# Strassen operands of h read back from a float32 copy in memory, and the softplus chain moved behind the second slab pair

## The chip, the core and the metric

The kernel runs on one core of a Trainium2 chip. The metric is device time in microseconds (us). Five engines work side by side, each through its own list of instructions and strictly in that list's order: TensorE (PE: matmuls, with its weight loads shown as PEld), VectorE (DVE), ScalarE (ACT), GpSimd (POOL) and SyncE (SP), which here issues every transfer between memory and the chip. An instruction whose data is not there yet holds up everything behind it in its own list. The profile was taken from one execution of the kernel before the change.

## What is computed

One layer of a decoder trunk, for 1024 tokens (S) of width 1024 (D):

```
h      = rmsnorm(x, norm_w) * (1 + scale) + shift        # scale, shift from c
proj   = h @ w_in                                        # 1024 x 8472
z_ssm, xbc, dt_raw, q, k, v, z_att, f_logit, g_logit = split(proj)
dt     = softplus(dt_raw + dt_bias)                      # SSD branch, 16 heads
log_f  = log_sigmoid(f_logit + b_f)                      # attention branch, 8 heads
y_ssm  = ssd(silu(conv(xbc)), dt, ...) gated by z_ssm
y_att  = softmax attention with cumsum(log_f) gated by z_att
out    = rmsnorm(x + gate * ((g_ssm * y_ssm@Wp + g_att * y_att@Wa) @ Wo))
```

All of it is float32. TensorE multiplies a rounded form (fp32r), so each operand is split into a rounded part "hi" and a rest "lo", and a product is three matmuls: hi*hi, hi*lo, lo*hi.

## The kernel before

**First phase (L202 to L326).** x is normalised, transposed on TensorE in half tiles of 128 by 512 (L302), and turned into h by ScalarE (`xa`, L305). `xa` is then split: ScalarE casts the rounded part `hh` (L306), VectorE subtracts to get `hl` (L307). Eight tiles k = 0..7 of D, two halves each. The scale and shift come from matrix-vector products that VectorE does as chains of 128x256 multiply-adds on `w_ada` (L287, L289). TensorE uses `hh` and `hl` at once for three slabs of the gate projection (L115 to L117).

**Second phase (L607 to L614).** `v_slab(0)` computes two heads of v and, in 24 more columns, the raw dt and f values (L140 to L142); eight small VectorE copies (L348) take these columns out of the PSUM banks into `tmp`. `t_forms(k)`, k = 0..3, builds Strassen sums of h: four blocks of h (two of tile k, two of tile k+4) are made by adding `hh` and `hl` (L440: eight adds on VectorE, eight on GpSimd), four VectorE subtractions combine them (L441 to L444), and each result is split again (L102 cast on ScalarE, L103 subtraction on VectorE or GpSimd) into the tiles `tha, tla, thb, tlb`. `gate_slab(3)` is one more plain slab. Then `dt_chain` evaluates the softplus for all 24 columns: 28 VectorE instructions on 128x192 values with one ScalarE exponential, ending in two small TensorE matmuls (L393, L394) that sum over time; `ssm_sums` does the sums for the SSD branch (L401 to L427).

**Slab pairs (L616 to L627).** The other 34 slabs of the projection are done in pairs n = 0..16. A pair of slabs is one 2x2 Strassen product: seven products f1, f6, f7, f5, f4, f2, f3, each of 12 matmuls of 128x512, instead of eight. f1 and f2, f3 use `hh, hl`; f6 and f4 use `thb, tlb`; f7 and f5 use `tha, tla`. The weight sums are VectorE subtractions (L477 to L480), each followed by a cast (ScalarE) and a subtraction (GpSimd, L103). The results are combined by VectorE reading PSUM (L504 to L517). Pair 1 is a pair of convolution slabs: behind its products VectorE runs eight 128x1024 instructions (L538, L541, L544). `WPREP` says ahead of which pair the Strassen sums of later weights are prepared (`w_sums`, L586 to L594).

The eight PSUM banks are three `mm` and five `pp` tiles. The instructions are put in order when the program is built, by a scheduler that follows the code's order as its priority and hands out the tiles of a pool in the order in which the code asks for them. So a `pp` bank that a later product needs is only given out after the `pp` bank that an earlier statement asked for.

Of the kernel before, what the change touches and what calls it, by code (L numbers as in the profile page):

```python
# [31 lines left out]
P = 128  # L32
S = 1024
D = 1024
NK = 8
# [17 lines left out]
OOUT = (1, 2, 6, 7, 5, 4, 3)  # L53
WV = {'ps': (), 'pa': (1,), 'o': (1, 2, 3)}
WVI = (("o", 3),)
WPREP = {0: [('ps', 0)], 2: [('ps', 1)], 3: [('ps', 2)], 6: [('ps', 3), ('pa', 0)], 8: [('pa', 1)], 10: [('pa', 2), ('g', 0)], 12: [('pa', 3), ('g', 2), ('g', 3)], 11: [('g', 1)], 13: [('G', 0)], 15: [('o', 0)], 16: [('o', 1)], 17: [('o', 2)], 18: [('o', 3)]}
PREP = (6, 1, 0, 0, 0, 0, 0, 0, 1)
APRI, SPRI = 1000, 300
FILL = [[], [0, 2], [4, 5, 9], [1, 3, 6, 7, 8]]
# [10 lines left out]
def build(ctx, tc, t):  # L70
# [9 lines left out]
    def f32(ap):  # L80
        return ap.bitcast(F32)
# [120 lines left out]
    with tc.tile_pool(name="st", bufs=1, side="right") as st, \  # L202
# [95 lines left out]
        def h_half(k, hf):  # L298
            fs = slice(hf * 512, (hf + 1) * 512)
            tp = stp.tile([P, 512], F32, tag="tp", bufs=1, name="tp")  # L300
            for i in range(4):
                PE.transpose(out=tp[:, i * P:(i + 1) * P], in_=xts[4 * hf + i][:, k * P:(k + 1) * P],  # L302
                             identity=ident)
            xa = st.tile([P, 512], F32, tag="xa", bufs=4, name="xa")
            A.activation(out=xa, in_=tp, func=AF.Identity, scale=av[:, k:k + 1], bias=sv[:, k:k + 1])  # L305
            A.copy(out=hh[k][:, fs], in_=xa)  # L306
            V.tensor_tensor(out=hl[k][:, fs], in0=xa, in1=f32(hh[k][:, fs]), op=ALU.subtract)  # L307

# [24 lines left out]
    def gate_slab(j):  # L333
        evac, store = gate_out(j)
        c_slab(t["w_c"], G0 + j, hh, hl, evac)
        store()

    def v_slab(pair, dtf=None):
        vt = []

        def evac(tb, ps):
            per = ps.shape[1]
            g, i = tb // 4, tb % 4
            if i == 0:
                vt.append(ev("vt")[:, :1024].rearrange("p (i c) -> p i c", i=4))
            A.copy(out=vt[g][:, i:i + per, :], in_=ps[:, :, 0:256])
            if dtf is not None:
                V.tensor_copy(out=dtf[:, tb:tb + per, :], in_=ps[:, :, 256:280])  # L348
            if i + per == 4:
                SP.dma_start(out=v_scr[pair][g], in_=vt[g])  # L350

        if dtf is not None:
            with tc.issue_after(was["last"].ins):
                t_slab([t["w_v0"][u] for u in range(4)], 280, hh, hl, evac)
        else:
            t_slab([t["w_v"][pair - 1, u] for u in range(4)], 256, hh, hl, evac)
# [3 lines left out]
    with tc.tile_pool(name="pa", bufs=1, side="right") as pa, \  # L360
# [71 lines left out]
        def pe_tile():  # L432
            return pa.tile([P, 512], F32, tag="pe", bufs=4, name="pe")

        def t_forms(k):
            th1, tl1, th2, tl2 = (pa.tile([P, S], F32R, name=f"t{n}{k}") for n in ("ha", "la", "hb", "lb"))
            b11, b12, b21, b22 = (pe_tile() for _ in range(4))
            lo, hi = slice(0, 512), slice(512, 1024)
            for b, kk, hs, eng in ((b11, k, lo, V), (b12, k, hi, G), (b22, k + 4, hi, G), (b21, k + 4, lo, V)):
                eng.tensor_tensor(out=b, in0=f32(hh[kk][:, hs]), in1=f32(hl[kk][:, hs]), op=ALU.add)  # L440
            V.tensor_tensor(out=b11, in0=b12, in1=b11, op=ALU.subtract)  # L441
            V.tensor_tensor(out=b12, in0=b22, in1=b12, op=ALU.subtract)
            V.tensor_tensor(out=b22, in0=b22, in1=b11, op=ALU.subtract)
            V.tensor_tensor(out=b21, in0=b21, in1=b22, op=ALU.subtract)  # L444
            for b, th, tl, hs, eng in ((b11, th1, tl1, lo, V), (b12, th1, tl1, hi, G), (b22, th2, tl2, hi, V),
                                       (b21, th2, tl2, lo, G)):
                split(b, th[:, hs], tl[:, hs], 512, eng)
            tta.append((th1, tl1))
            ttb.append((th2, tl2))
# [157 lines left out]
        tmp = ev("tmp")  # L607
        dtf = tmp[:, 0:192].rearrange("p (c n) -> p c n", n=24)
        v_slab(0, dtf)
        for k in range(4):  # L610
            t_forms(k)
        gate_slab(3)
        dt_chain(dtf, tmp)
        ssm_sums()  # L614
        gb = None
        for n, (sa, sb) in enumerate(PAIRS):  # L616
            for wn, p in WPREP.get(n, ()):
                if wn == "g":
# [622 lines left out]
```

## Time and profile before

| | |
|---|---|
| median of 3 runs | 1285.14 us (1281.14 to 1290.57) |
| the profiled execution, its own time | 1286.09 us |
| its span, first to last instruction | 1284.4 us |
| mean granted TensorE clock | 0.974 |
| PE busy | 1183.9 us, 92% of the span |
| DVE busy | 963.1 us, 75% |
| POOL busy | 776.1 us, 60% |
| ACT busy | 594.8 us, 46% |

TensorE is the engine that is nearly always busy, so time is lost where TensorE waits. A row of a timeline gives the start, the duration, engine, line and operation, and in brackets the idle time ahead of it with the instruction that ended this idle time. A row of windows gives for each engine the busy time (and the count of instructions) in a stretch. Stretches here are in us from the span's start.

### The profile page before, as it was taken

How to read it: one execution, taken by the hardware profiler on the slowest of the kernel's cores; microseconds unless marked ns; L12 is line 12 of the kernel's file. 1: busy time of each engine (PE TensorE's matmuls, PEld its weight loads, DVE VectorE, ACT ScalarE, POOL GpSimd, SP SyncE). 2: the span in 40 equal slices, each digit the busy share in tenths (PEclk: the TensorE clock that was granted, in tenths of full speed). 3: DMA queues.
4: the chain of work that ended last, by engine and by line, in shares of the span. 5: the costliest groups of instructions: out<-in, count | busy, mean ns of one | idle time of the engine just before them, and what ended most of it. 6: DMA issues, size and time to landing. Idle time of an engine off the chain costs nothing. (4 is left out here: it accounts for less than half of the span.)

```text
span 1284.4 us, 18783 instructions
## 1 busy us (share of the span) xinstructions
PE 1183.9 (92%) x6206; PEld 988.8 (77%) x6206; DVE 963.1 (75%) x1618; ACT 594.8 (46%) x1194; POOL 776.1 (60%) x644
## 2 busy tenths in 40 slices
PE   4897899999978999999988999999999999999896
PEld 3686688777766788799778888888887787878685
DVE  6979767787799566348689764545667968999997
ACT  5443324242423232477667733444456553444354
POOL 3258465474755476448887966435446635587666
PEclk9998899998989999999999999999999999999999
DMA  8422443624556566654565558623236619766143
GB/s 346 158 100 98 160 123 124 213 64 167 188 185 216 175 211 228 223 177 148 188 200 163 173 191 296 210 87 116 74 127 210 201 55 328 224 188 193 52 116 145
DMA packets 104126, 219.70 MB, mean 171 GB/s; under 512 B 11818, under 2 KB 19420, under 8 KB 103004
## 3 DMA queue, kind: packets, MB, share of 16 engines
q1 hardware_dynamic: 104028, 218.50, 51.5%
q8 instruction: 49, 0.80, 0.3%
q14 instruction: 49, 0.40, 0.1%
HBM read 154.85 MB, written 63.61 MB: 170 GB/s over the span
## 5 line engine op out<-in xcount | busy, mean ns | idle before, releaser
L103 POOL TENSOR_TENSOR wl<-wr,wh 128x512 fp32r<-128x512 f32 (+1 forms) x188 | 281.5, 1508 | 135.7 <-ACT wh L102 130.7
L102 ACT CAST wh<-wr 128x512 fp32r<-128x512 f32 (+1 forms) x214 | 129.8, 618 | 158.4 <-DMA wr<-w_c 53.7
L103 POOL TENSOR_TENSOR sl<-sr,sh 128x512 fp32r<-128x512 f32 x57 | 91.0, 1603 | 78.8 <-ACT sh L102 65.7
L115 PE MATMUL mm<-hh,wh 128*128 128x512 f32 x288 | 115.9, 407 | 4.3 <-ACT wh L102 1.9
L116 PE MATMUL mm<-hl,wh 128*128 128x512 f32 x288 | 116.7, 405 | 3.0 <-DVE hl L307 3.0
L117 PE MATMUL mm<-hh,wl 128*128 128x512 f32 x288 | 116.3, 405 | 0.0
L102 ACT CAST sh<-sr 128x512 fp32r<-128x512 f32 x57 | 34.1, 619 | 96.6 <-DVE sr L478 77.0
L140 PE MATMUL mm<-wh,hh 128*128 128x256 f32 (+1 forms) x256 | 74.9, 294 | 3.8 <-DVE tmp L348 3.8
L141 PE MATMUL mm<-wl,hh 128*128 128x256 f32 (+1 forms) x256 | 74.8, 293 | 0.0
L142 PE MATMUL mm<-wh,hl 128*128 128x256 f32 (+1 forms) x256 | 74.4, 292 | 0.0
L1018 ACT ACTIVATE pr<-pr,sm 128x1024 f32<-128x1024 f32 (+3 forms) x64 | 49.9, 780 | 50.4 <-DVE sm L1017 42.4
L1021 POOL TENSOR_SCALAR pr<-pr,sm 128x1024 f32<-128x1024 f32 (+3 forms) x64 | 48.6, 762 | 34.7 <-DVE sm L1020 30.2
L1013 DVE CUSTOM_DVE_ANT_0 pr<-lg,fb 128x512 f32<-128x512 f32 (+1 forms) x96 | 51.5, 551 | 23.5 <-PE lg L1012 14.0
L115 PEld LDWEIGHTS mm<-hh,wh 128*128 128x128 f32 x288 | 55.1, 193 | 15.6 <-ACT wh L102 2.4
L116 PEld LDWEIGHTS mm<-hl,wh 128*128 128x128 f32 x288 | 55.3, 192 | 14.7 <-DVE hl L307 3.9
L1004 POOL TENSOR_SCALAR_AFFINE_SELECT fb<-fb 128x128 f32<-128x128 f32 x64 | 21.9, 344 | 72.1 <-DVE sm L1013 57.3
L117 PEld LDWEIGHTS mm<-hh,wl 128*128 128x128 f32 x288 | 55.2, 192 | 10.8
L1037 DVE TENSOR_TENSOR ptl<-tp,pth 128x512 fp32r<-128x512 f32 (+1 forms) x80 | 50.1, 632 | 15.9 <-ACT pth L1036 15.5
L1036 ACT CAST pth<-tp 128x512 fp32r<-128x512 f32 (+1 forms) x80 | 42.3, 543 | 41.5 <-PE tp L1033 32.4
L683 ACT ACTIVATE ab<-ab,acs 128x128 f32<-128x128 f32 x128 | 41.1, 391 | 31.7 <-DMA ab<-a_scr 28.1
L140 PEld LDWEIGHTS mm<-wh,hh 128*128 128x128 f32 x256 | 49.5, 194 | 4.7 <-DVE tmp L348 4.5
L103 POOL TENSOR_TENSOR m<-ab,m 128x512 fp32r<-128x512 f32 x32 | 46.7, 1462 | 7.1 <-ACT m L102 4.7
(393 smaller groups left out, 3972.6 us busy)
## 6 DMA issues: line engine op xcount, KB each, us to landing
wr<-w_c SPq DMA_DIRECT2D x116, 256.0 KB, 3.5
wa<-w_ada SPq DMA_DIRECT2D x8, 1024.0 KB, 11.4
g_scr<-gt SPq DMA_DIRECT2D x16, 512.0 KB, 4.0
ab<-a_scr SPq DMA_DIRECT2D x32, 256.0 KB, 3.7
gt<-g_scr SPq DMA_DIRECT2D x32, 256.0 KB, 3.0
wr<-w_ps SPq DMA_DIRECT2D x28, 256.0 KB, 2.9
wr<-w_pa SPq DMA_DIRECT2D x28, 256.0 KB, 3.1
wr<-so SPq DMA_DIRECT2D x28, 256.0 KB, 2.6
```

What stands on the lines that cost most here:

```text
L102: A.copy(out=hi[:, :n], in_=raw[:, :n])
L103: eng.tensor_tensor(out=lo[:, :n], in0=raw[:, :n], in1=f32(hi[:, :n]), op=ALU.subtract)
L115: PE.matmul(ps, lhsT=hi[:, cs], rhs=xh[k][:, hs], start=(k == 0), stop=False)
L116: PE.matmul(ps, lhsT=hi[:, cs], rhs=xl[k][:, hs], start=False, stop=False)
L117: PE.matmul(ps, lhsT=lo[:, cs], rhs=xh[k][:, hs], start=False, stop=(k == 7))
L140: PE.matmul(o, lhsT=xh[k][:, ts], rhs=hi[:, cs], start=(k == 0), stop=False)
L141: PE.matmul(o, lhsT=xh[k][:, ts], rhs=lo[:, cs], start=False, stop=False)
L142: PE.matmul(o, lhsT=xl[k][:, ts], rhs=hi[:, cs], start=False, stop=(k == 7))
L1013: V.tensor_tensor_reduce(out=pr[:, n0:n1], in0=lg[:, :n1 - n0], in1=fb[:, n0:n1], op0=ALU.add, op1=ALU.min, scale=1.0, scalar=BIG, accum_o ...
L1018: A.activation(out=pr[:, :n], in_=pr[:, :n], func=AF.Exp, scale=-1.0, bias=sm[:, 0:1], accum_out=sm[:, 1:2])
L1021: G.tensor_scalar(out=pr[:, :n], in0=pr[:, :n], scalar1=sm[:, 1:2], scalar2=0.5, op0=ALU.mult, op1=ALU.mult)
L1037: V.tensor_tensor(out=ptl[:, :w], in0=tp[:, :w], in1=f32(pth[:, :w]), op=ALU.subtract)
```

## The change

Five edits, all before the third slab pair:

- ScalarE's `xa` is also stored to a float32 copy of h in memory, `h_scr` (16 transfers of 256 KB).
- `t_forms` loads its four blocks from `h_scr` (16 transfers of 256 KB) in place of the 16 adds. For odd k the four blocks sit in buffers of the pool `sh` instead of `pe`.
- `gate_slab(3)` stands ahead of `t_forms`.
- The raw dt and f columns are stored to `d_scr`; `dt_chain` is called ahead of pair 2 on a copy that is loaded back, and `ssm_sums` ahead of pair 3.
- The first `w_sums` goes from pair 0 to pair 1.

```
-WPREP = {0: [('ps', 0)], 2: [('ps', 1)], ...
+WPREP = {1: [('ps', 0)], 2: [('ps', 1)], ...
...
+    h_scr = [dram.tile([P, S], F32, name=f"h_scr{k}") for k in range(NK)]
+    d_scr = dram.tile([P, 192], F32, name="d_scr")
...
             A.activation(out=xa, in_=tp, func=AF.Identity, scale=av[:, k:k + 1], bias=sv[:, k:k + 1])
+            SP.dma_start(out=h_scr[k][:, fs], in_=xa)
             A.copy(out=hh[k][:, fs], in_=xa)
...
         def t_forms(k):
-            b11, b12, b21, b22 = (pe_tile() for _ in range(4))
+            b11, b12, b21, b22 = (pe_tile() if k % 2 == 0 else pa.tile([P, 512], F32, tag="sh", bufs=SB[1], name="sb")
+                                  for _ in range(4))
             lo, hi = slice(0, 512), slice(512, 1024)
-            for b, kk, hs, eng in ((b11, k, lo, V), (b12, k, hi, G), (b22, k + 4, hi, G), (b21, k + 4, lo, V)):
-                eng.tensor_tensor(out=b, in0=f32(hh[kk][:, hs]), in1=f32(hl[kk][:, hs]), op=ALU.add)
+            for b, kk, hs in ((b12, k, hi), (b11, k, lo), (b22, k + 4, hi), (b21, k + 4, lo)):
+                SP.dma_start(out=b, in_=h_scr[kk][:, hs])
...
         v_slab(0, dtf)
+        SP.dma_start(out=d_scr, in_=tmp[:, 0:192])
+        gate_slab(3)
         for k in range(4):
             t_forms(k)
-        gate_slab(3)
-        dt_chain(dtf, tmp)
-        ssm_sums()
         gb = None
         for n, (sa, sb) in enumerate(PAIRS):
+            if n == 2:
+                tmp = ev("tmp")
+                SP.dma_start(out=tmp[:, 0:192], in_=d_scr)
+                dt_chain(tmp[:, 0:192].rearrange("p (c n) -> p c n", n=24), tmp)
+            if n == 3:
+                ssm_sums()
```

In the changed file the lines of the first phase stand 2 to 3 lower, those of `dt_chain` 3 (L393 is L396 there, L387 is L390) and those of the pairs 4 lower (L504 is L508, L541 is L545). The text below goes by the numbers of the kernel before.

The change also moves instructions in the engines' lists. Three places follow, of before and of the change apart.

TensorE's list around the first matmul of `dt_chain` (its operand is `tmp`), before: it stands inside the products of pairs 0 and 1 (`tha` with `wl` is f7 of pair 0, `thb` with `sh` into `mm` is f6 of pair 1, `tha` with `sh` into `pp` is f5 of pair 0).

```order
L497 MATMUL mm<-tha_1134,wl 128x512
L495 MATMUL mm<-thb_1064,sh 128x512
L393 MATMUL pp<-tri,tmp 64x128
L496 MATMUL mm<-tlb_1065,sh 128x512
L409 MATMUL pp<-a,tri 128x128
L410 MATMUL pp<-a,ones 128x128
L411 MATMUL pp<-tri,a 128x128
L495 MATMUL pp<-tha_1062,sh 128x512
L394 MATMUL pp<-ones,tmp 64x128
```

The same matmul after the change (L396), behind f7, f5 and f4 of pair 2 and ahead of f1 of pair 2.

```order
L499 MATMUL mm<-thb_1228,wh 128x512
L500 MATMUL mm<-tlb_1229,wh 128x512
L501 MATMUL mm<-thb_1228,wl 128x512
L396 MATMUL pp<-tri,tmp 64x128
L499 MATMUL pp<-hh_240,wh 128x512
L500 MATMUL pp<-hl_248,wh 128x512
L501 MATMUL pp<-hh_240,wl 128x512
```

So f1, f6, f2 and f3 of pair 2 now stand behind a matmul that needs the value written by L387 (L390 there), near the end of `dt_chain`; f7, f5 and f4 of pair 2 have gone ahead of them.

VectorE's list behind the last combination of pair 1 (L517), before: the convolution's instructions stand between those that combine pair 2 (L504 to L511).

```order
L517 TENSOR_TENSOR pp<-pp,pe 128x512
L477 TENSOR_TENSOR sr<-wr 128x512
L538 TENSOR_SCALAR cv<-xp,cols 128x1024 x2
L478 TENSOR_TENSOR sr<-sr,wr 128x512
L479 TENSOR_TENSOR wr<-wr 128x512
L541 SCALAR_TENSOR_TENSOR cv<-xp,cols,cv 128x1024 x2
L480 TENSOR_TENSOR sr<-wr,sr 128x512
L504 TENSOR_TENSOR pe<-pp,pe 128x512
L541 SCALAR_TENSOR_TENSOR cv<-xp,cols,cv 128x1024 x2
L505 TENSOR_TENSOR pe<-mm,pe 128x512
```

The same place after the change: from the combination (L521 is L517 of before) to the start of the softplus chain (L372 is L369).

```order
L521 TENSOR_TENSOR pp<-pp,pe 128x512
L591 TENSOR_TENSOR sr<-sr,wr 128x512
L542 TENSOR_SCALAR cv<-xp,cols 128x1024 x2
L545 SCALAR_TENSOR_TENSOR cv<-xp,cols,cv 128x1024 x4
L481 TENSOR_TENSOR sr<-wr 128x512
L545 SCALAR_TENSOR_TENSOR cv<-xp,cols,cv 128x1024 x2
L482 TENSOR_TENSOR sr<-sr,wr 128x512
L483 TENSOR_TENSOR wr<-wr 128x512
L548 SCALAR_TENSOR_TENSOR cv<-xp,cv 128x1024
L484 TENSOR_TENSOR sr<-wr,sr 128x512
L548 SCALAR_TENSOR_TENSOR cv<-xp,cv 128x1024
L372 TENSOR_TENSOR tmp<-tmp,hb 128x192
```

All of the convolution, then the whole chain, now precede the first combination of pair 2 (L508 there, not yet in these rows). The `tmp` of the chain takes the buffer of a convolution input, so its load too comes behind the first L544.

VectorE's list in the first phase, before: the `hl` of tile 4 (`hh_235`), and how many multiply-adds on `w_ada` still follow it.

```order
L307 TENSOR_TENSOR hl_243<-xa,hh_235 128x512
L289 SCALAR_TENSOR_TENSOR acc<-wa,cols,acc 128x256 x2
L307 TENSOR_TENSOR hl_243<-xa,hh_235 128x512
L289 SCALAR_TENSOR_TENSOR acc<-wa,cols,acc 128x256 x2
L307 TENSOR_TENSOR hl_244<-xa,hh_236 128x512
L289 SCALAR_TENSOR_TENSOR acc<-wa,cols,acc 128x256 x4
L307 TENSOR_TENSOR hl_244<-xa,hh_236 128x512
L289 SCALAR_TENSOR_TENSOR acc<-wa,cols,acc 128x256
```

After the change (L310 is L307, `hh_244` is tile 4, `hh_245` tile 5), down to the first instruction of `t_forms`.

```order
L291 SCALAR_TENSOR_TENSOR acc<-wa,cols,acc 128x256 x3
L310 TENSOR_TENSOR hl_252<-xa,hh_244 128x512
L296 SCALAR_TENSOR_TENSOR av<-cp,cols 128x1
L298 TENSOR_TENSOR sv<-cp,cols 128x1
L310 TENSOR_TENSOR hl_252<-xa,hh_244 128x512
L310 TENSOR_TENSOR hl_253<-xa,hh_245 128x512 x2
L310 TENSOR_TENSOR hl_254<-xa,hh_246 128x512 x2
L310 TENSOR_TENSOR hl_255<-xa,hh_247 128x512 x2
L445 TENSOR_TENSOR pe<-pe 128x512
```

The nine multiply-adds that followed the first `hl` of tile 4 now precede it.

More of the change, by code (lines that the diff above doesn't have):

```diff
@@ L55 @@
 WVI = (("o", 3),)
-WPREP = {0: [('ps', 0)], 2: [('ps', 1)], 3: [('ps', 2)], 6: [('ps', 3), ('pa', 0)], 8: [('pa', 1)], 10: [('pa', 2), ('g', 0)], 12: [('pa', 3), ('g', 2), ('g', 3)], 11: [('g', 1)], 13: [('G', 0)], 15: [('o', 0)], 16: [('o', 1)], 17: [('o', 2)], 18: [('o', 3)]}
+WPREP = {1: [('ps', 0)], 2: [('ps', 1)], 3: [('ps', 2)], 6: [('ps', 3), ('pa', 0)], 8: [('pa', 1)], 10: [('pa', 2), ('g', 0)], 12: [('pa', 3), ('g', 2), ('g', 3)], 11: [('g', 1)], 13: [('G', 0)], 15: [('o', 0)], 16: [('o', 1)], 17: [('o', 2)], 18: [('o', 3)]}
 PREP = (6, 1, 0, 0, 0, 0, 0, 0, 1)
```

## The prediction

> **What bounds the kernel now.** I read the engines' totals first, then windows of 20 us over the changed stretch, then the timelines of TensorE and VectorE there. The page's total, and behind it the windows (start:end, length, busy us and count for PE, PEld, DVE, ACT, POOL, then granted clock, DMA share, GB/s):
>
> ```profile
> PE 1183.9 (92%) x6206; PEld 988.8 (77%) x6206; DVE 963.1 (75%) x1618; ACT 594.8 (46%) x1194; POOL 776.1 (60%) x644
> ```
>
> ```profile
> 60.00:80.00 20.00, 20.00 (x111) 17.13 (x110) 9.86 (x17) 9.02 (x14) 3.43 (x2) 0.99 0.00 1
> 80.00:100.00 20.00, 16.52 (x124) 15.84 (x123) 18.85 (x18) 8.64 (x18) 17.19 (x11) 1.00 0.64 217
> 100.00:120.00 20.00, 16.18 (x76) 13.95 (x77) 19.28 (x22) 7.13 (x14) 16.18 (x10) 0.83 0.15 50
> 120.00:140.00 20.00, 15.28 (x59) 11.65 (x57) 19.76 (x27) 7.92 (x14) 13.71 (x11) 0.91 0.35 111
> 140.00:160.00 20.00, 18.64 (x77) 14.70 (x78) 12.49 (x31) 5.97 (x11) 8.85 (x7) 0.91 0.57 196
> 160.00:180.00 20.00, 20.00 (x89) 16.21 (x88) 9.64 (x13) 7.08 (x12) 11.99 (x9) 1.00 0.50 159
> ```
>
> TensorE is full up to 80 us and again from 160. From 80 to 160 it is busy 66.62 of 80, so 13.4 us are idle, and VectorE is busy 18.85 to 19.76 of 20 up to 140: there VectorE bounds the kernel, with `t_forms` and `dt_chain`. TensorE's timeline gives the marks:
>
> ```profile
> 56.58 0.50 PE L116 MATMUL mm<-hl,wh 128*128 128x512 f32 x1 [2.31 <-DVE hl L307]
> 79.33 0.39 PE L117 MATMUL um<-hh,e 128*128 128x512 f32 x1
> 100.34 0.40 PE L140 MATMUL mm<-wh,hh 128*128 128x280 f32 x1 [3.02 <-DVE tmp L348]
> 113.00 0.50 PE L115 MATMUL mm<-hh,wh 128*128 128x512 f32 x1 [1.93 <-ACT wh L102]
> 131.53 0.50 PE L495 MATMUL mm<-thb,sh 128*128 128x512 f32 x1 [3.87 <-ACT gt L186]
> 132.41 0.63 PE L495 MATMUL mm<-thb,sh 128*128 128x512 f32 x1
> 134.97 0.63 PE L495 MATMUL mm<-thb,sh 128*128 128x512 f32 x1
> 135.39 0.52 PE L496 MATMUL mm<-tlb,sh 128*128 128x512 f32 x1
> 141.36 0.43 PE L393 MATMUL pp<-tri,tmp 128*64 128x128 f32 x2 [2.21 <-DVE tmp L387]
> 155.94 0.39 PE L495 MATMUL pp<-hh,wh 128*128 128x512 f32 x1
> 156.17 0.39 PE L496 MATMUL pp<-hl,wh 128*128 128x512 f32 x1
> 174.69 0.39 PE L497 MATMUL pp<-hh,sl 128*128 128x512 f32 x1
> 194.09 0.40 PE L497 MATMUL pp<-hh,sl 128*128 128x512 f32 x1
> ```
>
> 156.17 - 155.94 gives the pitch, 0.23 us per 128x512 matmul (a modelled end makes a row longer). Pair 1 runs from 155.94 to 174.92 (19.0), pair 2 to 194.32 (19.4): 84 matmuls at 0.23, no gap. A gate slab of 48 is 11.2, a product of 12 is 2.8.
>
> **The change part by part.** All on the profiled execution's own time, 1286.09, which is 0.95 above the median of the three runs.
>
> *First phase.* Nine multiply-adds of L289 move ahead of the first `hl` of tile 4. VectorE's rows:
>
> ```profile
> 56.45 0.87 DVE L289 SCALAR_TENSOR_TENSOR acc<-wa,cols,acc 128x256 f32<-128x256 f32 x2
> 77.85 1.78 DVE L441 TENSOR_TENSOR pe<-pe 128x512 f32<-128x512 f32 x1
> 80.98 0.68 DVE L443 TENSOR_TENSOR pe<-pe 128x512 f32<-128x512 f32 x1
> 81.70 1.80 DVE L444 TENSOR_TENSOR pe<-pe 128x512 f32<-128x512 f32 x1
> 117.64 1.25 DVE L369 TENSOR_TENSOR tmp<-tmp,hb 128x192 f32<-128x192 f32 x1
> 134.43 0.35 DVE L379 SCALAR_TENSOR_TENSOR tmp<-tmp 128x192 f32<-128x192 f32 x1
> 175.12 0.70 DVE L517 TENSOR_TENSOR pp<-pp,pe 128x512 f32<-128x512 f32 x1 [2.10 <-PE pp L497]
> 178.58 1.10 DVE L477 TENSOR_TENSOR sr<-wr 128x512 f32<-128x512 f32 x1 [2.77 <-DMA wr<-w_c]
> 192.47 1.27 DVE L541 SCALAR_TENSOR_TENSOR cv<-xp,cols,cv 128x1024 f32<-128x1024 f32 x1
> 197.85 4.00 DVE L544 SCALAR_TENSOR_TENSOR cv<-xp,cv 128x1024 f32<-128x1024 f32 x2
> ```
>
> Nine at 0.45 (0.87 for two, with little overlap) are 4.1 us. TensorE already waits 2.31 for this `hl` at 56.58 and has no gap from there to 79.56, so all of it lands on the path: the phase ends near 83.7.
>
> *Loads in place of adds.* The 16 stores hold back nothing but SP, whose DMAs idle in that window (share 0.00 in 60:80). Four rows price the step: ScalarE's last `xa`; VectorE's group of adds (busy us, mean ns); the `pe` tiles alone in 75.5:128.4 (DVE, ACT, POOL); and the nearest transfers of 256 KB, a load and a store, with the median us from issue to landing.
>
> ```profile
> 73.28 0.78 ACT L305 ACTIVATE xa<-tp,sv,av 128x512 f32<-128x512 f32 x1 [1.10 <-PE tp L302]
> ```
>
> ```profile
> L440 DVE TENSOR_TENSOR pe<-hh,hl 128x512 f32<-128x512 f32 x8 | 12.9, 1627 | 1.2 <-POOL tlb L103 1.1
> ```
>
> ```profile
> 75.50:128.40 52.90, 38.09 (x32) 9.83 (x16) 25.30 (x16) 0.94 0.36 120
> ```
>
> ```profile
> wr<-w_ps SPq DMA_DIRECT2D x16, 256.0 KB, 2.5
> sps<-wr SPq DMA_DIRECT2D x4, 256.0 KB, 2.4
> ```
>
> The loads go into a pool that opens when the first phase's pool is free, its last store included. So: 74.06, plus 4.1, plus 2.4, plus a load of 2.5 to 3 with its issue and a second behind it, is 84.3 for the first L441 (77.85 now). Bounds for this step: 2.4 + 2.5 and twice that. VectorE's list then holds 26 subtractions and splits and eight small copies up to the last split. The `pe` instructions without the adds are 38.09 - 12.9 = 25.2 us for 24, 1.05 each. So 26 take 27.3, the copies (0.17 each) 1.4: the last `tlb` is at about 115, where it is 128.2 today.
>
> TensorE meanwhile: `v_slab(0)` is eight blocks, one per PSUM bank, on three banks.
>
> ```profile
> L140 PE MATMUL mm<-wh,hh 128*128 128x280 f32 x64 | 19.3, 307 | 3.8 <-DVE tmp L348 3.8
> ```
>
> 64 of L140 with as many of L141 and L142 are 192 matmuls, at 0.23 x 280/512 = 0.13 some 3.1 us a block. Three blocks end at 93.0. The fourth needs the first L348, which now stands behind ten instructions of `t_forms`: 84.3 + 10.5 + 0.2 = 95.0. The other copies stand early enough, so block eight ends at 110.5. The gate slab is 11.2 and, with about 2 us of waits as in 113.00's row, ends near 124. One restart is slow: behind the wait of 3.87 the pitch is 0.43 from 132.41 to 135.39, which costs 1.7. Pair 0 (19.5) then ends at 145.2 where it ended at 155.94: **10.7 us gained**. Without any wait behind the first phase it would be 83.7 + 24.8 + 11.2 + 19.5 = 139.2, a gain of 16.7 (and 21 if the first phase did not grow either); with the late end of the load step and VectorE at 1.3 per instruction it is 5.
>
> *The chain behind pair 1.* Call t0 the end of pair 1, 174.92 now, 164.2 after. TensorE's list then has f7, f5 and f4 of pair 2, 36 matmuls or 8.4 us, and then L393, which waits for L387. It can't be passed: at 141.36 the same matmul held TensorE 2.21 us. Behind it are 48 matmuls of pair 2 and all pairs. On VectorE stand, from t0 to L387: L517, L587, two L538, six L541, L477 to L480 (four), two L544, then 17 instructions of the chain with L477 and L479 of pair 4 and one exponential on ScalarE (0.37 in the first row below). None is done early: the convolution needs L517, and the chain's `tmp` load needs a convolution input's buffer, free only behind L544.
>
> The `tmp` instructions in 117.60:141.40 (PE, PEld, DVE, ACT), and the `cv` ones in 175:202 (DVE, ACT):
>
> ```profile
> 117.60:141.40 23.80, 0.04 (x1) 0.04 (x1) 14.86 (x22) 0.37 (x1) 0.91 0.38 122
> ```
>
> ```profile
> 175.00:202.00 27.00, 15.54 (x10) 2.12 (x2) 1.00 0.30 92
> ```
>
> Two prices exist for each, and POOL's row beside VectorE's at 80.98 and 81.70 shows when:
>
> ```profile
> 80.97 3.70 POOL L103 TENSOR_TENSOR wl<-wr,wh 128x560 fp32r<-128x560 f32 x2 [1.89 <-ACT wh L102]
> ```
>
> The subtraction that began as POOL left its idle time took 0.68, the next, beside POOL, 1.80; L379 and its like are 1.25 or 0.35; L541 is 1.27 at 192.47, and L544 is 2.00 at 197.85. Clean, the convolution part is 0.7 + 0.7 + 2 x 0.8 + 6 x 1.27 + 4 x 0.7 + 2 x 1.25 = 15.9; as in 175.12 to 201.85 it is 26.7 less six combinations of pair 2 (4.1) and the wait of 2.77 for a weight, some 20. Clean, the chain is 17 x 0.35 + 1 for the reciprocal + 0.8 for ScalarE + 1.4 = 9; as measured 14.86 + 2.2 = 17. I take 18.5 for the first and 9 for the second, 27.5 in all (ends 25 and 37): POOL has work while the weights' buffers fill, and little once TensorE stands still, since those buffers come free only by products. At t0 + 8.4 TensorE stops and waits 19 us. The clock then restarts (1.7), L393 and L394 take 0.9, four products 11.2: pair 2 ends at t0 + 41.3, against t0 + 19.5 without a wait. **21.8 us lost.**
>
> [...]
>
> *The rest.* `w_sums` of pair 0 goes to pair 1 with the same instructions, where VectorE is busy 9.64 of 20 (160:180): nothing, or 1.7 if it holds a combination. `ssm_sums` ahead of pair 3 leaves its L409 behind a short VectorE instruction: 0 to 1. The `d_scr` store waits in SP's list for the last L348, with weight loads behind it, which are not needed before 118: nothing. From pair 4 on the order is as before. Later waits could absorb some of the lateness, TensorE's longest after 200 us being:
>
> ```profile
> PE mm L495 <- ACT gt L186: 7.3, 1, 7.3
> ```
>
> It hangs on work of its own pair, so I take nothing, with 2 us as the likely bound.
>
> **Sum.** 1286.1 - 10.7 + 21.8 = 1297.2 on the profiled execution, **1296** against the median. With the gain between 5 and 16 and the loss between 19 and 25 it lies between 1288 and 1305.
>
> **Rivals.**
>
> A, the gain covers the loss (not slower): VectorE no longer holds TensorE in `t_forms` at all, since the adds were a third of its `pe` time. Pair 0 ends at 135 to 139, and the chain runs at its clean end (25). Gain 17 to 21, loss 19.3: 1283 to 1287. For it: 12.9 us leave the engine that was full. Against: the load step starts 6.5 us later than the adds, and the first L348 is behind it. It decides if the first L441 comes before about 80, or if the copies L348 run ahead of it.
>
> B, the chain stays contended: it runs at 14.86 + 2.2 as before and the convolution at 20, L387 comes at t0 + 37, TensorE waits 28.5, and the loss is 31.3: 1306. For it: 14.86 us is what the chain took with POOL busy 13.71 of 20 (120:140), and POOL is busy 11.99 in 160:180. Against: POOL runs out of work in a stall. [...]
>
> C, the lateness is absorbed later: the wait of 7.3 above and as much again in smaller ones go, 14, while the early gain stands at 11 to 21: 1270 to 1283. The pairs keep their order, so a wait on a pair's own ScalarE work does not shrink.
>
> D, the change doesn't do what it says: L387 is ready when TensorE reaches L393. It would need 28 us of VectorE work in 8.4, and is under 1 in 100.
>
> **How the numbers follow.** Chances: the forecast 0.50, A 0.21, B 0.23, C 0.05, D under 0.01. One per cent of 1285.14 is 12.9 us, about what a measurement of this kernel can tell from no change: faster is under 1272.3, slower over 1298.0. Of the forecast 0.30 lies under 1298 and 0.20 above; A is all "same"; B is all "slower"; C gives 0.04 "faster" and 0.01 "same", with D on "faster". Together faster 0.05, same 0.52, slower 0.43. The range leaves out C and the far end of B: 1280 to 1309. The forecast's own is 1288 to 1305.
>
> **What would show it.** TensorE busy less than 10 of 20 in the window behind pair 1, with one wait at L393's successor for L387 of 17 to 21 us; pair 0 ending at 141 to 150; first `hl` wait of 6.4 instead of 2.31; VectorE's `t_forms` from 84 to 115. A wait under 12 us there, or pair 0 ending before 138, makes the forecast wrong on the low side; a wait over 25, or pair 0 after 151, on the high side.

## The result and the profile after

| | before | after |
|---|---|---|
| median of 4 runs beside each other | 1287.82 us | 1303.80 us (1302.24 to 1304.72) |
| ratio, 95% interval | | 1.0133 (1.0111 to 1.0156) |
| the profiled execution: own time, span | 1286.09, 1284.4 us | 1302.24, 1300.5 us |
| PE busy | 1183.9 us | 1182.4 us |
| DVE busy | 963.1 us | 934.5 us |
| POOL busy | 776.1 us | 759.7 us |

The change made the kernel 1.3% slower, although VectorE and GpSimd do less. Lines are those of the changed kernel below: L396 is L393 of before, L390 is L387, L351 is L348, L521 is L517, and L590, L591 are the first two instructions of the weight sums.

The windows of the changed kernel, in the columns of the prediction:

```profile
80.00:100.00 20.00, 15.13 (x101) 14.65 (x100) 12.69 (x16) 8.68 (x17) 9.44 (x6) 0.91 0.90 307
100.00:120.00 20.00, 20.00 (x131) 18.58 (x131) 14.76 (x20) 9.20 (x20) 12.58 (x9) 1.00 0.24 80
120.00:140.00 20.00, 20.00 (x88) 16.26 (x87) 6.86 (x11) 6.44 (x12) 11.24 (x9) 1.00 0.61 197
140.00:160.00 20.00, 20.00 (x87) 16.14 (x86) 7.59 (x15) 5.84 (x11) 11.26 (x9) 1.00 0.59 198
160.00:180.00 20.00, 10.82 (x47) 8.45 (x45) 14.83 (x15) 4.18 (x9) 11.29 (x9) 0.85 0.50 157
180.00:200.00 20.00, 2.84 (x7) 2.13 (x8) 15.56 (x35) 4.40 (x7) 6.08 (x3) 0.50 0.30 97
200.00:220.00 20.00, 20.00 (x87) 15.89 (x86) 7.54 (x18) 8.09 (x15) 7.00 (x6) 0.97 0.25 88
```

The hole that lay in 80 to 160 (13.4 us of idle TensorE) has shrunk to 4.87, and a larger one stands in 160 to 200, where TensorE is busy 13.66 of 40. TensorE's timeline has one cause for it:

```profile
95.21 0.41 PE L140 MATMUL mm<-wh,hh 128*128 128x280 f32 x1 [4.87 <-DVE tmp L351]
123.39 0.40 PE L499 MATMUL mm<-hh,wh 128*128 128x512 f32 x1
142.84 0.40 PE L499 MATMUL pp<-hh,wh 128*128 128x512 f32 x1
162.35 0.39 PE L499 MATMUL mm<-tha,wh 128*128 128x512 f32 x1
197.16 0.69 PE L396 MATMUL pp<-tri,tmp 128*64 128x128 f32 x2 [26.34 <-DVE tmp L390]
198.37 0.63 PE L500 MATMUL pp<-hl,wh 128*128 128x512 f32 x1
201.36 0.43 PE L501 MATMUL pp<-hh,wl 128*128 128x512 f32 x1
211.26 0.39 PE L499 MATMUL mm<-tha,sh 128*128 128x512 f32 x1
```

Pair 0 ran from 123.39 to 142.84 (it ended at 155.94 before), pair 1 ended at 162.35 (174.92 before), and then TensorE, with f7, f5 and f4 of pair 2 done, waited 26.34 us for L390. Pair 2 ended at 211.26 instead of 194.32. So TensorE was 12.6 us early at one end of pair 2 and 16.9 us late at the other, and the span has grown by 16.1: hardly anything was made up later.

What VectorE did in these 34.8 us, from the end of pair 1 (162.35) to the end of L390:

```profile
167.10 0.69 DVE L590 TENSOR_TENSOR sr<-wr 128x512 f32<-128x512 f32 x1 [5.17 <-DMA wr<-w_ps]
167.71 0.69 DVE L521 TENSOR_TENSOR pp<-pp,pe 128x512 f32<-128x512 f32 x1
168.31 1.46 DVE L591 TENSOR_TENSOR sr<-sr,wr 128x512 f32<-128x512 f32 x1
169.69 2.49 DVE L542 TENSOR_SCALAR cv<-xp,cols 128x1024 f32<-128x1024 f32 x2
172.10 5.87 DVE L545 SCALAR_TENSOR_TENSOR cv<-xp,cols,cv 128x1024 f32<-128x1024 f32 x4
...
183.82 1.21 DVE L548 SCALAR_TENSOR_TENSOR cv<-xp,cv 128x1024 f32<-128x1024 f32 x1
186.92 0.67 DVE L372 TENSOR_TENSOR tmp<-tmp,hb 128x192 f32<-128x192 f32 x1 [1.89 <-DMA tmp<-d_scr]
...
193.72 2.33 DVE L382 SCALAR_TENSOR_TENSOR tmp<-tmp 128x192 f32<-128x192 f32 x6
...
196.87 0.23 DVE L390 TENSOR_SCALAR tmp<-tmp 128x64 f32<-128x64 f32 x1
```

To 167.10 it waited for a weight that the sums now at pair 1 need, 4.75 us past the end of pair 1; 2.6 us went to the last combination and the sums; the convolution took 169.69 to 185.03 (15.3; GpSimd stood idle for 9.34 of it, up to 182.63), the wait for the load of `tmp` 1.9, the chain 186.92 to 197.10 (10.2).

### The profile page after: what moved, and what is told of

Read it like the earlier page. It is cut to its first block, busy times and chain, and to the rows that moved or that the text cites. A ratio compares the mean times of both kernels' runs of the same rounds, so it can differ in the third digit from the quotient of the medians.

```text
span 1300.5 us, 18848 instructions
## 1 busy us (share of the span) xinstructions
PE 1182.4 (91%) x6206; PEld 988.6 (76%) x6206; DVE 934.5 (72%) x1610; ACT 594.6 (46%) x1194; POOL 759.7 (58%) x636
## 5 line engine op out<-in xcount | busy, mean ns | idle before, releaser
L103 POOL TENSOR_TENSOR wl<-wr,wh 128x512 fp32r<-128x512 f32 (+1 forms) x188 | 280.2, 1502 | 166.6 <-ACT wh L102 149.8
L103 POOL TENSOR_TENSOR sl<-sr,sh 128x512 fp32r<-128x512 f32 x57 | 91.1, 1605 | 87.4 <-ACT sh L102 74.6
L1022 DVE CUSTOM_DVE_ANT_0 pr<-lg,fb 128x512 f32<-128x512 f32 (+1 forms) x96 | 51.6, 551 | 21.5 <-PE lg L1021 13.1
L116 PEld LDWEIGHTS mm<-hl,wh 128*128 128x128 f32 x288 | 55.4, 192 | 13.4 <-DVE hl L310 2.6
L117 PEld LDWEIGHTS mm<-hh,wl 128*128 128x128 f32 x288 | 55.3, 192 | 10.9
L1046 DVE TENSOR_TENSOR ptl<-tp,pth 128x512 fp32r<-128x512 f32 (+1 forms) x80 | 50.1, 632 | 17.9 <-ACT pth L1045 17.6
L115 PEld LDWEIGHTS mm<-hh,wh 128*128 128x128 f32 x288 | 54.8, 193 | 10.4 <-DVE ql L972 0.6
L1045 ACT CAST pth<-tp 128x512 fp32r<-128x512 f32 (+1 forms) x80 | 42.4, 543 | 40.5 <-PE tp L1042 31.3
L141 PEld LDWEIGHTS mm<-wl,hh 128*128 128x128 f32 x256 | 49.4, 193 | 0.2
```

The source lines that it names most:

```text
L103: eng.tensor_tensor(out=lo[:, :n], in0=raw[:, :n], in1=f32(hi[:, :n]), op=ALU.subtract)
L115: PE.matmul(ps, lhsT=hi[:, cs], rhs=xh[k][:, hs], start=(k == 0), stop=False)
L116: PE.matmul(ps, lhsT=hi[:, cs], rhs=xl[k][:, hs], start=False, stop=False)
L117: PE.matmul(ps, lhsT=lo[:, cs], rhs=xh[k][:, hs], start=False, stop=(k == 7))
L141: PE.matmul(o, lhsT=xh[k][:, ts], rhs=lo[:, cs], start=False, stop=False)
L1022: V.tensor_tensor_reduce(out=pr[:, n0:n1], in0=lg[:, :n1 - n0], in1=fb[:, n0:n1], op0=ALU.add, op1=ALU.min, scale=1.0, scalar=BIG, accum_o ...
```

## Experiments

Two numbers are read from each run beside its time: TensorE's wait for the chain, and the **lead**, how much earlier (-) or later (+) than in the kernel before VectorE starts the last combination of a pair (L521). It is worked out by taking the start of each L521 in the run's timeline less that of its counterpart in the kernel before; the profiled executions stand for it, one of each kernel. It is VectorE's lead: TensorE can be further ahead. Five kernels whose code up to the end of pair 0 is the same (chain_only, c25, c1314, c1415, c1516) stand 10.6 to 13.2 us early there, so leads that differ by 2 or 3 us are not told apart. Short names are the labels of the runs.

| run | pair 0 | 1 | 2 | 3 | 4 | 8 | 12 | 14 | 18 |
|---|---|---|---|---|---|---|---|---|---|
| the changed kernel | -13.1 | -7.4 | +7.9 | +18.8 | +16.9 | +15.1 | +15.5 | +16.4 | +14.7 |
| h_only | -2.9 | -1.1 | -4.9 | -2.9 | -3.0 | -2.7 | -3.3 | -1.4 | -1.1 |
| chain_only | -12.3 | -11.8 | +4.7 | +13.7 | +12.3 | +11.8 | +10.4 | +11.0 | +9.3 |
| wprep_back | -13.4 | -12.8 | +4.5 | +13.5 | +12.2 | +11.7 | +11.0 | +10.5 | +8.3 |
| mm_n3 | -12.8 | -6.5 | -12.0 | +7.8 | +6.6 | +5.2 | +5.5 | +6.9 | +4.6 |
| late25 | -13.2 | -7.7 | -13.1 | +1.1 | -1.7 | +1.2 | +3.1 | -1.0 | +3.8 |
| c25 | -10.8 | -10.3 | -12.6 | -2.3 | -5.0 | -3.4 | -2.4 | -6.1 | -1.3 |
| c1314 | -10.6 | -10.1 | -12.8 | -10.9 | -10.8 | -11.0 | -11.6 | -4.0 | -7.4 |
| c1415 | -11.6 | -10.8 | -13.2 | -11.1 | -11.2 | -10.8 | -11.5 | -8.9 | -5.9 |
| c1516 | -13.2 | -12.7 | -14.9 | -12.9 | -13.0 | -12.5 | -12.2 | -12.2 | -4.3 |

### The two halves of the change apart

**h_only**: the copy of h and the earlier gate slab stay, the chain goes back.

```
-        SP.dma_start(out=d_scr, in_=tmp[:, 0:192])
         gate_slab(3)
         for k in range(4):
             t_forms(k)
+        dt_chain(dtf, tmp)
+        ssm_sums()
...
-            if n == 2:
-                tmp = ev("tmp")
-                SP.dma_start(out=tmp[:, 0:192], in_=d_scr)
-                dt_chain(tmp[:, 0:192].rearrange("p (c n) -> p c n", n=24), tmp)
-            if n == 3:
-                ssm_sums()
```

> The changed kernel with the softplus chain and the SSD sums put back ahead of pair 0, straight on tmp; the float32 copy of h and the earlier gate slab stay. Theory (the whole loss is the wait of TensorE for L390 behind pair 1, the copy of h is a gain): no wait for L390 over 3 us, pair 0 ends at 142 to 146 (142.84 in the changed kernel, 155.94 before), pair 2 about 38 us later without a gap; time 1273 to 1277, ratio to before 0.988 to 0.992. Rival (the copy of h pays only because the chain has left that stretch: VectorE is full again): pair 0 ends at 150 or later, 1283 or more.

Measured: 1285.19 us against 1286.01, ratio 0.9984 (0.9956 to 1.0011): no difference is shown. The theory missed its range, and the rival's was met. Pair 0's last combination is only 2.9 us earlier, 10 less than in the changed kernel. TensorE's timeline of this run shows where most of these 10 us went:

```profile
94.44 0.60 PE L140 MATMUL mm<-wh,hh 128*128 128x280 f32 x1 [4.88 <-DVE tmp L351]
132.86 0.43 PE L396 MATMUL pp<-tri,tmp 128*64 128x128 f32 x2 [3.30 <-DVE tmp L390]
135.56 0.69 PE L397 MATMUL pp<-ones,tmp 128*64 128x128 f32 x2 [1.30 <-DVE tmp L394]
136.77 0.63 PE L500 MATMUL mm<-tla,wh 128*128 128x512 f32 x1
141.04 0.63 PE L501 MATMUL mm<-tha,wl 128*128 128x512 f32 x1
```

The chain holds TensorE 4.6 us, and behind it the clock is low to 141.04 (a pitch of 0.43, against 0.23; the clock granted over 120:140 is 0.87, in the row below), which costs an estimated 2.4 more for 12 matmuls. VectorE's window says why:

```profile
120.00:140.00 20.00, 15.36 (x61) 11.73 (x60) 18.87 (x38) 5.25 (x11) 9.35 (x9) 0.87 0.59 192
```

VectorE is full (18.87 of 20) with the chain where the adds used to fill it.

**chain_only**: the kernel before with the chain alone moved.

```
+        SP.dma_start(out=d_scr, in_=tmp[:, 0:192])
         for k in range(4):
             t_forms(k)
         gate_slab(3)
-        dt_chain(dtf, tmp)
-        ssm_sums()
...
+            if n == 2:
+                tmp = ev("tmp")
+                SP.dma_start(out=tmp[:, 0:192], in_=d_scr)
+                dt_chain(tmp[:, 0:192].rearrange("p (c n) -> p c n", n=24), tmp)
+            if n == 3:
+                ssm_sums()
```

> The kernel before with the chain alone moved (raw columns through d_scr, chain ahead of pair 2, SSD sums ahead of pair 3); the 16 adds, the order of the gate slab and the place of the weight sums stay. Theory: the same wait behind pair 1, 18 to 26 us; early gain only 4 to 8, since the chain's 15 us leave a stretch that the adds still fill; pair 2 ends 14 to 24 later than before; time 1302 to 1312, ratio 1.011 to 1.019. Rival (the chain's place costs little, the loss is the loads and stores of h): 1280 to 1290.

Measured: 1301.54 us, ratio 1.0117 (1.0079 to 1.0154); the wait is there:

```profile
PE pp L394 <- DVE tmp L388: 22.5, 1, 22.5
```

(L394 and L388 are this kernel's numbers for the same two.) The loss is the chain's move, as the theory had it (its range for the time, 1302 to 1312, is missed by 0.5). The early gain was not 4 to 8 but 12.3 us at pair 0, with all 16 adds in place. So the gain, too, is the chain's move: with the copy of h as well it is 13.1, a difference too small to be told, and the copy by itself (h_only) brings 2.9 there and no gain in the time that these runs can show.

### What the 34.8 us are made of

**wprep_back**: the changed kernel with `WPREP = {0: [('ps', 0)], ...}` again.

> The changed kernel with the first weight sums back at pair 0. Theory (of the 34.8 us from the end of pair 1 to L390, 4.75 are VectorE waiting at L590 for a weight of those sums, ahead of the last combination of pair 1): that wait goes, the wait of TensorE shrinks from 26.3 to 20 to 23, time 1297 to 1301. Rival (the chain's own contention or the convolution makes the extra length): the wait stays at 25 or more, time 1302 to 1306.

Measured: 1299.94 us, ratio to before 1.0106 (1.0067 to 1.0145), 3.9 us under the changed kernel, which four executions of each, spread over 1298.08 to 1305.30 here, do not settle. In the profiled executions the later pairs are 3 to 6 us less late (11.7 against 15.1 at pair 8). TensorE's wait for L390 shrank to 23.7, where 20 to 23 was expected, because VectorE now waits for another weight ahead of the convolution. Its timeline in this run:

```profile
162.27 0.70 DVE L521 TENSOR_TENSOR pp<-pp,pe 128x512 f32<-128x512 f32 x1 [0.98 <-PE pp L501]
166.99 1.11 DVE L481 TENSOR_TENSOR sr<-wr 128x512 f32<-128x512 f32 x1 [4.02 <-DMA wr<-w_c]
168.03 1.52 DVE L542 TENSOR_SCALAR cv<-xp,cols 128x1024 f32<-128x1024 f32 x2
...
186.58 0.36 DVE L372 TENSOR_TENSOR tmp<-tmp,hb 128x192 f32<-128x192 f32 x1 [1.49 <-DMA tmp<-d_scr]
...
193.96 0.23 DVE L390 TENSOR_SCALAR tmp<-tmp 128x64 f32<-128x64 f32 x1
```

The last combination is on time, and then VectorE waits 4.02 us for a weight of the pairs. Behind pair 1 some weight is late in all three of these kernels: 2.77 us before the change (L477), 4.02 here, 5.17 in the changed kernel. So the chain starts only 0.3 us earlier than in the changed kernel (186.58 against 186.92). What TensorE's wait lost, 2.6 us, is the chain itself, 7.6 us long here against 10.2: it holds no weight subtraction, and its first two instructions take 0.36 and 0.20 us where they took 0.67 and 1.14 beside GpSimd's L103. This run doesn't show, then, that the moved weight sums are what made VectorE wait there. In the changed kernel SyncE, which issues the loads, waited 5.6 us, in three waits between 160 and 200, for GpSimd's L103 to free buffers for the weights of these sums; whether that sets their time was not tried.

**no_taps**: the convolution of pair 1's two slabs without its three taps, so that six of its ten instructions on VectorE, and their part of the output, are left out.

```
-                for i in range(1, 4):
+                for i in range(1, taps + 1):
...
-                return conv_out(s - XB0)
+                return conv_out(s - XB0, 0 if s - XB0 in (8, 9) else 3)
```

> The changed kernel without the three taps of the convolution in the two slabs of pair 1 (six of the eight L541, 8.3 us of VectorE behind pair 1; those channels of the output are then wrong). Theory (L390 comes after a plain sum of VectorE's list): the wait of TensorE ahead of pair 2's f1 shrinks from 26.3 by 8 to 9, to 17 to 19, and the span by as much, 1290 to 1293. Rival (the weights' loads or the clock set the wait): under 4 us less.

Measured: the wait is 20.1 (from 26.3) and the span 1293.6, which is 6.9 less (one execution). Both are just outside the theory's ranges and far from the rival's. Of the 8.3 us taken out, 1.0 came back as a wait for a weight behind the convolution, 1.0 in the two L548, and 1.4 in a longer chain (its first and third instructions took 1.43 and 1.38 instead of 0.67 and 0.36; what slowed them there is not shown); the wait of 1.9 for the load of `tmp` went. L390 stands at the end of a plain sum of VectorE's list, and TensorE's wait follows this sum.

### Is it the matmul or VectorE?

**mm_n3**: VectorE's part of the chain stays, its two matmuls go ahead of pair 3.

```
+        def dt_mm(tmp):
             ps = pap.tile([P, 512], F32, tag="pp", bufs=5, name="pp")
             PE.matmul(ps[0:64, 0:P], lhsT=tmp[:, 192:256], rhs=tri, start=True, stop=False)
...
             if n == 3:
+                dt_mm(tmp)
                 ssm_sums()
```

> The changed kernel, with only the two matmuls of the chain (L396, L397) and what follows them put ahead of pair 3; VectorE's part of the chain keeps its place in the code ahead of pair 2. Theory (the matmul that waits, and the bank it asks for, is what stops TensorE): f1, f6, f2 and f3 of pair 2 no longer wait; one wait of 2 to 7 us ahead of pair 3 where the matmul is now; time 1278 to 1285. Rival (VectorE's backlog of convolution and chain stops TensorE anyway, through banks not emptied): a wait of 15 us or more in pair 2 or 3, time 1293 or more.

Measured: 1291.16 us, ratio 1.0037 (1.0012 to 1.0062), between the two ranges. Pair 2 no longer waits for the chain (lead -12.0 at its end, against +7.9), so the matmul is what stopped it. But three waits follow:

```profile
185.33 0.80 PE L500 MATMUL mm<-tha,sh 128*128 128x512 f32 x1 [3.10 <-ACT sh L102]
188.38 0.79 PE L502 MATMUL mm<-tha,sl 128*128 128x512 f32 x1 [1.82 <-POOL sl L103]
208.00 0.69 PE L399 MATMUL pp<-tri,tmp 128*64 128x128 f32 x2 [10.12 <-DVE tmp L390]
```

The matmul (L399 here) waits again, 10.1 us, now ahead of pair 3, with VectorE busy 19.73 of 20 in 180:200.

**late25, c25, late25w**: the matmuls and the SSD sums are put off to pair 5, with the chain's result in `dec`. late25 is the changed kernel so treated, c25 the kernel before (adds and all), late25w is late25 with the first weight sums at pair 0.

```
+        lfp = dec.rearrange("p c h -> p (c h)")
...
-            lf = tmp[:, 192:256].rearrange("p (h c) -> p h c", h=8)
+            lf = lfp[:, 0:64].rearrange("p (h c) -> p h c", h=8)
...
-            if n == 3:
+            if n == 5:
+                dt_mm()
                 ssm_sums()
```

> The changed kernel, with VectorE's part of the chain where the changed code has it (ahead of pair 2) and its two matmuls, with the SSD sums, ahead of pair 5; the chain's result waits in the tile dec, which is free by then. Theory (what costs is a matmul and its PSUM bank in TensorE's list ahead of its value; VectorE's work as such fits): no wait of TensorE for L390 or what is made of it, waits of at most 3 to 8 us in all in pairs 2 to 4, most of the early gain of 12 to 13 us is kept; time 1276 to 1281, ratio 0.991 to 0.996. Rival (VectorE's backlog of chain plus convolution is what costs): the waits only change their name, 1288 or more.

> The kernel before with the same treatment of the chain (VectorE's part ahead of pair 2, matmuls ahead of pair 5) and none of the other edits: the 16 adds stay. Theory A (the early gain is the chain's leaving, as pair 0 ended at 143.85 with the chain alone moved and at 143.04 with everything): within 2 us of the run with the copy of h, 1275 to 1281. Theory B (the prediction's: the adds' 12.9 us were half of it): 1282 or more.

> As the first of these runs, with the first weight sums back at pair 0. Theory (those sums at pair 1 put VectorE behind a weight load that lands late, 4.0 us when the chain was gated): 2 to 4 us faster than the first run, if the delay of the last combination of pair 1 still reaches TensorE; the same time if the delay is hidden now. Time 1273 to 1280.

Measured: late25 1292.25 us, ratio 1.0051 (1.0032 to 1.007), where the rival said 1288 or more; c25 1287.74, 1.0008 (0.9988 to 1.0028); late25w 1288.71, 1.0021 (1.0000 to 1.0041). All three missed the theory's times. c25 has the time of its theory B (1282 or more), but not by B's mechanism: pair 0 is 10.8 us early with all the adds in place. late25w is 3.5 us faster than late25, within the 2 to 4 expected, but none is faster than before. No wait for the chain is left, and VectorE's lead is lost all the same, between pairs 2 and 3 (-13.1 to +1.1, -12.6 to -2.3). TensorE loses its own in one wait (17.4 us in late25), which in c25 follows the two matmuls:

```profile
223.25 0.38 PE L400 MATMUL pp<-ones,dec 128*64 128x128 f32 x2
236.75 0.80 PE L499 MATMUL mm<-hh,wh 128*128 128x512 f32 x1 [13.12 <-DVE zt L529]
```

VectorE's read of the `mm` bank in c25 that ended it, and the windows of c25:

```profile
236.02 0.67 DVE L529 SCALAR_TENSOR_TENSOR zt<-zt,mm 128x512 f32<-128x512 f32 x1
```

```profile
180.00:200.00 20.00, 20.00 (x88) 16.21 (x88) 18.02 (x25) 9.64 (x16) 17.34 (x11) 1.00 0.58 185
200.00:220.00 20.00, 20.00 (x88) 16.27 (x87) 19.59 (x33) 5.95 (x11) 9.65 (x8) 1.00 0.16 52
220.00:240.00 20.00, 6.88 (x26) 5.08 (x25) 18.89 (x22) 5.52 (x8) 9.72 (x5) 0.67 0.47 162
```

VectorE has little room there (18.0, 19.6, 18.9 of 20): the chain pushes back pair 3's combinations and convolution, so the PSUM bank that pair 4's results hold is read late (L529), and TensorE stands 13 us for it. The theory that only a matmul ahead of its value costs has fallen: VectorE's time in this stretch counts too.

How much of the 13 us is VectorE's is not settled, since the matmuls and the SSD sums ahead of pair 5 also change TensorE's list. Behind them stand two products into `mm` banks, and the first product of pair 5 into a `pp` bank follows at 244.71, behind the matmuls of the sums (L413 to L415). In c1415 (below), where neither the chain nor these matmuls are near, TensorE goes straight on into a `pp` bank:

```profile
222.06 0.39 PE L499 MATMUL pp<-hh,wh 128*128 128x512 f32 x1
```

The same L529 of VectorE starts there 6.2 us earlier:

```profile
229.85 0.67 DVE L529 SCALAR_TENSOR_TENSOR zt<-zt,mm 128x512 f32<-128x512 f32 x1
```

So some 6 of the 13 us are, by this estimate, the chain on VectorE, and the rest may be the new order. No run moves one without the other.

### Where the chain does no harm

If VectorE's time and the matmuls' place are all that costs, the lead must hold as long as the chain is not in the way. **c1415, c1314, c1516** are c25 with the chain ahead of pair 14, 13 or 15 and its matmuls one pair later; **late1415w** is c1415 with the copy of h and the earlier gate slab.

```
-            if n == 2:
+            if n == 14:
                 tmp = ev("tmp")
...
-            if n == 5:
+            if n == 15:
                 dt_mm()
```

> The kernel before with VectorE's part of the chain ahead of pair 14 and its matmuls, with the SSD sums, ahead of pair 15 (raw columns through d_scr, the result in dec); adds, gate slab and weight sums as before. Theory (an early TensorE needs VectorE to be as early: the chain's 10 to 15 us of VectorE cost that much in pairs 1 to 10, where VectorE is nearly full, and nothing from pair 12 on, where it is busy 8 to 14 of 20 us): pair 0 ends 11 to 13 us earlier than before, the lead is still 8 to 12 us at the last combination of pair 10, and the end comes 7 to 12 us earlier: 1274 to 1279, ratio 0.991 to 0.995. Rival (the lead cannot be held whatever is moved, since the pairs are paced by weights or by VectorE as they are): at most 3 us left at pair 5, 1283 or more.

> The same with VectorE's part ahead of pair 13 and the matmuls ahead of pair 14. Theory: the lead at pair 10 is the same 8 to 12 us; the chain now stands behind the gate sums (L565), where VectorE was busy 19.8 of 20 us in the kernel before, so it costs more than ahead of pair 14, up to 8 us: 1276 to 1284. Rival (as above): 1283 or more with at most 3 us of lead at pair 5.

> The changed kernel with the chain ahead of pair 14, its matmuls ahead of pair 15, and the first weight sums back at pair 0: against the first of these runs it differs by the float32 copy of h and the gate slab's place alone. Theory (with the chain gone from that stretch the copy of h is worth the 0.8 us that the end of pair 0 showed, since its loads land 5 us late): 1273 to 1279, within 3 us of that run. Rival (the adds' 12.9 us of VectorE and 13 of POOL count): 5 us or more faster than that run.

> The kernel before with the chain ahead of pair 15, its matmuls and the SSD sums ahead of pair 16. Theory (the lead of 11 us lasts until VectorE has to do the chain, and what is left then depends on the stretch it lands in): the lead is 11 us up to pair 14 (1 to 2 pairs longer than with the chain ahead of pair 14), 3 to 9 us at the end: 1278 to 1284, ratio 0.993 to 0.998. Rival (the lead is lost in pairs 13 to 16 by the gate products there, wherever the chain is): 4 us or less of lead left at pair 14.

| run | median | ratio to before, 95% interval |
|---|---|---|
| c1314 | 1279.88 us | 0.9949 (0.9930 to 0.9969) |
| c1415 | 1281.79 us | 0.9961 (0.9947 to 0.9976) |
| late1415w | 1283.09 us | 0.9960 (0.9944 to 0.9977) |
| c1516 | 1285.99 us | 0.9993 (0.9973 to 1.0013) |

The lead holds from pair 1 to pair 12, at 10 to 15 us in the three runs of the table of leads (late1415w: 7.4 at the least), to pair 14 in c1516, and each loses some of it where its chain stands (pair 13 on, 14 on, 15 on). The windows of c1415 where c25 stopped:

```profile
200.00:220.00 20.00, 20.00 (x88) 16.20 (x88) 16.59 (x16) 4.85 (x9) 9.85 (x7) 1.00 0.17 54
220.00:240.00 20.00, 20.00 (x88) 16.23 (x87) 17.04 (x24) 6.03 (x9) 10.23 (x6) 1.00 0.72 258
```

Without the chain VectorE is busy 16.6 and 17.0 there, and TensorE is full. A full VectorE alone does not stop TensorE: before the change it was busy 20.0 of 20 in 220:240, and TensorE had no wait there. Later the chain costs again, in c1415:

```profile
440.00:460.00 20.00, 16.49 (x64) 12.59 (x63) 19.93 (x29) 6.30 (x11) 13.95 (x10) 0.91 0.56 202
```

VectorE was busy 13.8 in this window before the change. The expectation that nothing is lost from pair 12 on was wrong, and c1415 and late1415w missed their times: of 11 us of lead, a gain of 5 to 7 us in time (0.4 to 0.5%) is left in the two better versions, and c1314, expected to be the worse of them (1276 to 1284, met), is no worse than c1415. c1314 has the lowest median here. It is faster than the kernel before and the changed kernel, and its interval overlaps that of c1415. c1516 kept its lead longest (12.2 at pair 14) and ends even. Part of it went in a wait for the chain itself, ahead of pair 16:

```profile
476.99 0.69 PE L399 MATMUL pp<-tri,dec 128*64 128x128 f32 x2 [6.55 <-DVE dec L390]
```

The rest was lost at the end of the pairs and behind them, and what took it there was not tried. late1415w and c1415 do not differ: when the chain is out of the way, the copy of h (with the earlier gate slab) is worth nothing that these runs can show.

## Why the prediction was right or wrong

The time of 1303.8 lies in the range (1280 to 1309), the forecast of 1296 was 8 us too low, and the kernel is slower by 1.3% where "within 1%" had the larger chance. Set against the medians of its own runs the change costs 16 us, and the sum gave 11.

**Right: the mechanism and the place of the loss, and the direction of both halves.** One wait at L396 for L390 behind pair 1, TensorE nearly empty there, then a restart at a low clock (0.43 pitch from 198.37 to 201.36, against 0.23), and an early gain ahead of it. The sum had 1.7 us for this restart, as behind the wait of 3.87 before the change; that a longer stop costs no more at its end was the author's assumption. Behind the 26.34 us it was an estimated 1.7 as well: the nine matmuls from 197.78 to 201.62 took 3.84 us, against 2.1 at 0.23. VectorE's early marks came out as said: first L445 at 84.21 (84.3 said), first L351 at 94.98 (95.0), last split of `t_forms` at 114.4 (115, though the terms given for it, 84.3 + 27.3 + 1.4, make 113.0).

On TensorE the terms were less good than their sum. The wait of 6.4 for the first `hl` did not come (it was 1.17), and the three blocks of `v_slab` were done at 90.3, not 93.0. TensorE then waited 4.87 us instead of 2, and the slow restart came there, where it cost an estimated 1.6 us. So block eight ended at 112.3 (110.5 said). The gate slab had none of the 2 us of waits and pair 0 no slow restart, so pair 0 ended at 142.84 and not 145.2, and the gain at t0 was 12.6, not 10.7. Errors of both signs met here.

**Wrong: the size of the loss, in the step "The chain behind pair 1".** The sum had L387 of before (L390) at t0 + 27.5; it came at t0 + 34.8, and the loss was 29.5 (48.9 from t0 to the end of pair 2, less 19.4) where 21.8 stood. The 7.3 us are, from the rows above:
- 4.75: VectorE waits at L590 for a weight. The step subtracted the 2.77 us wait for a weight that the same place showed in before, as if it would not come again, and "The rest" had the moved `w_sums` at "nothing, or 1.7 if it holds a combination". The wait held the last combination of pair 1, and all the convolution behind it.
- 1.9: VectorE waits behind the last L548 for the load of `tmp`, which SyncE issued at 183.75, when the first L548 was done. The step named this load as waiting for the buffer and gave it no time.
- 1.2: the chain, 10.2 where 9 stood. Its first two instructions ran beside GpSimd and took 0.67 and 1.14, against 0.36 and 0.20 in wprep_back.
- The convolution and what goes with it, without the wait, was 17.9 where 18.5 stood, and takes back 0.6.

wprep_back takes the moved sums away, and the first of these terms hardly shrinks: another weight is then 4.02 us late at the same place. So a late weight belonged in the sum with either order; why the weights are late there stays open.

**Nearly right in size, by another cause: the early gain.** The prediction drew it from the adds' leaving and the chain's leaving together, and weighed the adds' 12.9 us. chain_only shows 12.3 of the 13.1 us with the adds in place, h_only 2.9 with the adds gone. So the size came out near by luck. The loads that replace the adds took longer than the 2.5 to 3 us that were assumed. From issue to landing (median), in the first 320 us of the changed kernel:

```profile
pe<-h_scr SPq DMA_DIRECT2D x8, 256.0 KB, 4.4
sb<-h_scr SPq DMA_DIRECT2D x8, 256.0 KB, 5.3
```

**The rivals.** A, the gain covering the loss, had both wrong: 17 to 21 for a gain of 12.6, 19.3 for a loss of 29.5. B gave 1306, close to the time, and 31.3 for the loss, by a mechanism that did not happen: the chain did not stay beside a busy GpSimd. It took 10.2 us and not 17. L382 ran at 0.39 each (2.33 for six), where before the change three of the same line (L379) took 3.07, or 1.02 each, with GpSimd at work from 130.97 to 133.69:

```profile
130.84 3.07 DVE L379 SCALAR_TENSOR_TENSOR tmp<-tmp 128x192 f32<-128x192 f32 x3
```

In the changed kernel GpSimd stood idle for 14.27 us, up to this row:

```profile
202.98 1.32 POOL L103 TENSOR_TENSOR wl<-wr,wh 128x512 fp32r<-128x512 f32 x1 [14.27 <-ACT wh L102]
```

So GpSimd ran out of work in the stall, as the prediction held against B, and of the chain's instructions only the first two ran beside it. The rows give the two prices, 0.39 us with GpSimd idle and 1.02 with GpSimd at work; what makes the difference no run tried. C, lateness absorbed later, moved less than 1 us (16.9 late at the end of pair 2, 16.1 at the end). D fell with the wait itself.

## What to carry to other kernels

In a list that runs in order, a matmul that waits for a chain on another engine should stand where that chain has long ended (L396 held TensorE for 26.34 us here), and its price is the sum of that engine's whole list from the last point where both meet, the waits for loads in this list included. A wait seen at a place before a change is not to be taken out of the sum because the instruction is another: behind pair 1 a weight was late in three kernels (2.77, 4.02 and 5.17 us), though not the same one in all, and it held whichever instruction came first. And time gained early need not be kept: VectorE's lead fell from 12.6 to 2.3 us in c25, where VectorE, with the chain in its list, was busy 18.0, 19.6 and 18.9 of 20, and only from 13.2 to 11.1 between the same pairs in c1415, without the chain there. Before moving work into a later stretch, see whether its engine has room there, and which instructions of the leader's list it changes.

## What the runs showed of the hardware

One thing was not expected: single executions of the same program spread widely. The kernel before ran in 1280.05 to 1292.22 us in 19 executions beside each other. The granted clock goes with it only in part: it was 0.969 to 0.975 in the five longest and 0.974 to 0.978 in the five shortest. So a version that gains 6 us needs many executions to be told from it, and leads of single profiled executions behind pair 18 are not read to the microsecond here.
